# Encoder trunk on one core: the rotary angle arithmetic moves from the vector engine to Pool

## The chip, the cores and the metric

The kernel runs on one core of one Trainium2 chip. The metric is device time in microseconds of one execution. The engines are named as in the profile: PE (TensorE, matrix products), DVE (VectorE), ACT (ScalarE), POOL (GpSimd) and SP (SyncE, which issues most transfers). Each engine works through a queue of its own, in order; engines wait for each other through semaphores.

## The reference

Two layers; x is 512 tokens by 1024. Each layer mixes tokens (latent attention with rotary positions beside a gated convolution), attends to a memory of 256 rows, and ends in a gated feed-forward part. The change concerns the angles of the rotary positions:

```python
def rope_cos_sin(positions, dim):
    inv_freq = ROPE_BASE ** (-jnp.arange(0, dim, 2, dtype=jnp.float32) / dim)
    ang = positions.astype(jnp.float32)[..., None] * inv_freq
    return jnp.cos(ang), jnp.sin(ang)

def hybrid_mixer(x, cos, sin, ...):
    proj = x @ w_in + b_in
    c_q, c_kv, k_r, u = ...
    y_att = mla_group(c_q, c_kv, k_r, cos, sin, ...)
    y_conv = conformer_conv_group(u, ...)
    return jnp.concatenate([y_att, y_conv], axis=-1) @ w_o
```

Positions go up to 4606, so an angle has to be brought into one turn with more than float32's bits before a sine is taken. There are 16 angles for each of 512 positions, and the tables are used by both layers.

## The kernel before, in words

**Products.** Every float32 operand is split into a high and a low part (`whi`, `wlo`; `xTh`, `xTl`), and each product is three matmuls (`mm3`, L250 to L252). Weights arrive in a raw buffer (three of them), ACT casts the high part (L225, L304) and DVE (L226) or POOL (L312) subtracts it to get the low part. The raw buffer is free for the next fetch once the low part is made.

**Start of the program.** x comes in four tiles of 128 tokens. `transpose_x` (L412 to L422) turns a tile on PE, ACT makes `xTh` and DVE `xTl`. The gated unit's input projection is cut into eight blocks of 128 features. `blocks[0].first`, `blocks[1].first` and `blocks[2].first` compute blocks 0 to 2 for the first two token tiles (24 products of 128x256 each) as soon as these are there, while tiles 2 and 3 are still being turned; the second half of each block follows in the mixer. DVE splits the weights of blocks 0 to 2, POOL those of blocks 3 to 7 and of the latents (`wc`).

**Rotary tables.** `rope_tables` (L337 to L394) stands behind this. It casts the positions (`posi`, fetched by POOL's queue), multiplies them with 16 frequencies, splits the angle, multiplies it by 1/(2 pi) in parts of 12 bits and takes off whole turns by casting to integer and back (`whole`, L360 to L363). `tot` is then the angle in turns between -0.5 and 0.5. Seven more operations fold it for the sine and the cosine, and ACT takes `Sin` of both. All of it works on tiles `ropew` of 128x64 on DVE, each step on the result of the one before. POOL only fills in the frequencies.

**The mixer and its order.** The steps of layer 0's mixer are generators: each yields its engine, an estimated cost and the buffers and events that it needs. `Weave` is a list scheduler that emits them in the order in which it estimates that they could start. `issue_order` ties the instructions traced inside it to trace order on each engine; between the start and the mixer, which are two such sections, the tile framework may still interleave. Among the mixer's steps are the rest of the eight blocks (`gates`), the gate (ACT `th`, L650, then DVE `ch`, L652), the convolution with 31 taps on DVE (L616; one of four groups on ACT and POOL, L605 and L607), the transposes of the memory rows `mem` (L537), fetched by SP between the weights, and the latents (`latent`), which first use the tables (L711).

**Constants of a layer.** `mixer` begins with the fetches of `vec` and `cbias` on POOL's queue and with `hvec`, half of some of `vec` (L579 to L586).

Of the kernel before, what the change touches and what calls it, by code (L numbers as in the profile page):

```python
# [8 lines left out]
F32 = mybir.dt.float32  # L9
# [8 lines left out]
P = 128  # L18
# [25 lines left out]
SCRATCH = 9  # L44
POOL_TILES = (1,)
# [6 lines left out]
# ROPE_BASE ** (-arange(0, 32, 2) / 32) in float32  # L52
# [6 lines left out]
# 1 / (2 pi) in parts of 12 bits  # L59
TURN_BITS = 0x28BE60DB9391054A7F09  # floor(2**80 / (2 pi)), leading digits in hex  # L60
# [8 lines left out]
class Weave:  # L69
    """Emits the steps of several generators in the order in which a list scheduler would start them.  # L70

    A generator yields what its next step needs and emits that step when it is resumed. Steps of one generator
    follow each other; `get` and `put` count buffers, `wait` and `fire` order steps of different generators.
    """
# [82 lines left out]
@contextmanager  # L157
def issue_order(tc, engines):
    """Instructions traced inside are issued in trace order on each of the engines."""
    nc = tc.nc  # L160
    traced = nc.cur_bb.bb.instructions
    last = traced[-1]
    yield
    start = next(k for k in reversed(range(len(traced))) if traced[k] is last) + 1
    prev = {}
    for i in traced[start:]:
        if i.engine in engines:
            if i.engine in prev:
                tc.add_manual_dep(i, prev[i.engine].name,
                                  mybir.DependencyInfo(mybir.DependencyClass.NoSync, mybir.DependencyReason.DATA),  # L170
                                  reason="issue order")
            prev[i.engine] = i
# [3 lines left out]
def encoder(ctx: ExitStack, tc: tile.TileContext, x_in, mem_in, pos_in, wu, wc, wuq, wukv, wo,  # L176
# [45 lines left out]
    def split(src, hi, lo, scale=None):  # L222
        """hi + lo == src (times scale), hi and lo of 12 significant bits each."""
        if scale is None:
            nc.scalar.copy(hi, src)  # L225
            nc.vector.tensor_tensor(lo, src, hi.bitcast(F32), op=ALU.subtract)  # L226
        else:
            nc.scalar.activation(hi, src, AF.Copy if isinstance(scale, float) else AF.Identity, scale=scale)
            nc.vector.scalar_tensor_tensor(out=lo, in0=src, scalar=scale, in1=hi.bitcast(F32),
                                           op0=ALU.mult, op1=ALU.subtract)  # L230
# [17 lines left out]
    def mm3(o, l, r, first, last):  # L248
        """o += l^T r for split operands; lo * lo is below float32's last bit."""
        nc.tensor.matmul(o, l[0], r[0], start=first, stop=False)  # L250
        nc.tensor.matmul(o, l[0], r[1], start=False, stop=False)  # L251
        nc.tensor.matmul(o, l[1], r[0], start=False, stop=last)  # L252
# [7 lines left out]
    def blk(i, n=P):  # L260
        return slice(i * n, (i + 1) * n)
# [20 lines left out]
    class Unit:  # L282
        """A piece of weights on its way: fetched, then split, lo on DVE or on Pool."""
# [50 lines left out]
    cosT = const.tile([P, NT, 16], F32, name="cosT")  # L334
    sinT = const.tile([P, NT, 16], F32, name="sinT")

    def rope_tables():  # L337
        posi = const.tile([P, NT], I32, name="posi")
        nc.gpsimd.dma_start(out=posi, in_=pos_in)
        posf = const.tile([P, NT], F32, name="posf")  # L340
        nc.vector.tensor_copy(posf, posi)
        work = bigt([P, 16, 64], F32, name="ropew")
        used = iter(range(16))

        def t64():
            return work[:, next(used), :]

        ang, freq = t64(), t64()
        for i in range(16):
            nc.gpsimd.memset(freq[:, i:i + 1], INV_FREQ[i])  # L350
        for t in range(NT):
            nc.vector.tensor_scalar(ang[:, blk(t, 16)], freq[:, 0:16], posf[:, t:t + 1], None, op0=ALU.mult)
        ah = small.tile([P, 64], F32R, name="ah", bufs=1)
        nc.vector.tensor_copy(ah, ang)
        al = t64()
        nc.vector.tensor_tensor(al, ang, ah.bitcast(F32), op=ALU.subtract)
        ahf = ah.bitcast(F32)
        n, m, pr = t64().bitcast(I32), t64(), t64()

        def whole(dst, src):  # L360
            nc.vector.tensor_copy(n, src)
            nc.vector.tensor_copy(m, n)
            nc.vector.tensor_tensor(dst, src, m, op=ALU.subtract)  # L363

        tiny = t64()
        nc.vector.tensor_scalar(tiny, ahf, TURN_PARTS[5], None, op0=ALU.mult)
        for src, i in ((al, 4), (ahf, 4), (al, 3), (al, 2), (ahf, 3)):
            nc.vector.scalar_tensor_tensor(out=tiny, in0=src, scalar=TURN_PARTS[i], in1=tiny,
                                           op0=ALU.mult, op1=ALU.add)
        tot = t64()  # L370
        for first, (src, i) in enumerate(((ahf, 0), (al, 0), (ahf, 1), (al, 1), (ahf, 2))):
            nc.vector.tensor_scalar(pr, src, TURN_PARTS[i], None, op0=ALU.mult)
            if first == 0:
                whole(tot, pr)
            else:
                whole(pr, pr)
                nc.vector.tensor_tensor(tot, tot, pr, op=ALU.add)
                whole(tot, tot)
        nc.vector.tensor_tensor(tot, tot, tiny, op=ALU.add)
        hop = t64()  # L380
        nc.vector.tensor_scalar(hop, tot, 0.5, None, op0=ALU.is_gt)
        nc.vector.tensor_tensor(tot, tot, hop, op=ALU.subtract)
        nc.vector.tensor_scalar(hop, tot, -0.5, None, op0=ALU.is_lt)
        nc.vector.tensor_tensor(tot, tot, hop, op=ALU.add)
        a1, a2 = t64(), t64()
        nc.vector.tensor_scalar(a1, tot, -1.0, 0.5, op0=ALU.mult, op1=ALU.add)
        nc.vector.tensor_tensor(a1, a1, tot, op=ALU.min)
        nc.vector.tensor_scalar(a2, tot, -1.0, -0.5, op0=ALU.mult, op1=ALU.add)
        nc.vector.tensor_tensor(a1, a1, a2, op=ALU.max)
        nc.scalar.activation(sinT.rearrange("p t f -> p (t f)"), a1, AF.Sin, scale=TWO_PI)  # L390
        nc.vector.tensor_scalar(a2, tot, -1.0, None, op0=ALU.mult)
        nc.vector.tensor_tensor(a2, a2, tot, op=ALU.min)
        nc.vector.tensor_scalar(a2, a2, 0.25, None, op0=ALU.add)
        nc.scalar.activation(cosT.rearrange("p t f -> p (t f)"), a2, AF.Sin, scale=TWO_PI)  # L394

# [47 lines left out]
    class Norm:  # L443
        """x <- LayerNorm(ALPHA x + y) of one token tile, y arriving in two halves."""
# [22 lines left out]
    class Block:  # L467
        """128 output features of x W, feature-major over all the tokens."""
# [28 lines left out]
    def tail(x, gb, half0, mm, blocks, keep=None):  # L497
        """Token tiles leave one by one: product, norm, transposes; the next blocks start on the first tiles."""
# [23 lines left out]
    mkv = [dram.tile([XH, P, 1024], F32, name=f"mkv{l}") for l in range(DEPTH)]  # L522

    def memory_kv(l, wk, wv, begin, stored):
        """Steps; wk and wv are weight units."""
# [51 lines left out]
    def mixer(l, xT, blocks, x_src):  # L577
        v = vecp.tile([P, 148], F32, name="vec")
        nc.gpsimd.dma_start(out=v, in_=vec[l])  # L579
        hv = vecp.tile([P, 136], F32, name="hvec")  # L580
# [4 lines left out]
        cbias = scr(name="cbias")  # L585
        nc.gpsimd.dma_start(out=cbias, in_=row[l, 6:7, 0:CIN].partition_broadcast(P))  # L586

        # depthwise causal convolution, summed in a PSUM bank
# [32 lines left out]
        # gated linear unit, twice its value  # L621
# [25 lines left out]
        def gated_steps(m):  # L647
# [12 lines left out]
                   q=2, gate=2)  # L660

        # latents, token-major
# [15 lines left out]
        def latent(t):  # L678
# [28 lines left out]
            yield pool(1.5, fire=roped[t])  # L707
# [35 lines left out]
        # keys of two heads, feature-major: own 64 rows, then rotary and mask rows  # L743
# [22 lines left out]
        # queries of two heads, token-major for the rotation, then feature-major  # L766
# [37 lines left out]
        # values, token-major  # L804
# [10 lines left out]
        # attention: one item is a query tile of one head, or of both while they share a bank  # L815
# [76 lines left out]
        # channel norm and swish of the convolution, a token tile at a time  # L892
# [225 lines left out]
    xs = dram.tile([SEQ, D], F32, name="xs")  # L1118
    blocks = mixer_blocks(0)
# [6 lines left out]
    with issue_order(tc, ORDERED):  # L1126
        for t in range(2):
            transpose_x(x[t], t, xT)
        blocks[0].first(xT)
        blocks[1].load()  # L1130
        transpose_x(x[2], 2, xT)
        blocks[1].first(xT)
        blocks[2].load()
        transpose_x(x[3], 3, xT)
        blocks[2].first(xT)
        rope_tables()
    for l in range(DEPTH):
        x, xT, blocks = mixer(l, xT, blocks, x_in if l == 0 else xs)
# [73 lines left out]
```

## Time and profile before

| what | value |
|---|---|
| runs | 1493.42, 1491.61 and 1491.92 us, median 1491.92 |
| profiled execution, from first to last instruction | 1492.6 us (this span is the time that the profile gives for it) |
| PE busy | 1452.6 us, 97% |
| DVE busy | 856.7 us, 57% |
| ACT busy | 597.8 us, 40% |
| POOL busy | 358.1 us, 24% |
| DVE in 25 to 50 us | 24.21 of 25 us |
| PE in 50 to 75 us | 16.15 of 25 us |

The shares are means over stages with different limits. Around the change, in the first 100 us, DVE is busy nearly all the time from 25 us on, and PE is not. A busy PE is not PE at its peak: matmuls overlap, so what counts is the distance from one start to the next.

### The profile page before, as it was taken

Reading aid. Unit: us, or ns where it says so; the run is one execution under the profiler, and the core shown is the slowest. Engines: PE = TensorE matmul, PEld = TensorE weight load, DVE = VectorE, ACT = ScalarE, POOL = GpSimd, SP = SyncE. Lnnn points to the kernel's source line nnn. Section 1 sums busy time; section 2 is a strip of 40 time slices with the busy share of each in tenths; the row PEclk is TensorE's granted clock in tenths of the full one; section 3 lists DMA queues with packets and bytes.
Section 4 is the critical chain, followed back from the end, with each engine's and each line's share of the span. In section 5 each row is a group of like instructions: output and inputs, shape, how many; then the busy total and the mean of one; then the engine's idle time right before and its main releaser. Section 6 shows DMA issues by size and latency. Waiting matters only on the chain.

```text
span 1492.6 us, 20901 instructions
## 1 busy us (share of the span) xinstructions
PE 1452.6 (97%) x8152; PEld 1255.0 (84%) x8152; DVE 856.7 (57%) x1313; ACT 597.8 (40%) x1152; POOL 358.1 (24%) x539
## 2 busy tenths in 40 slices
PE   8799999999999999999999999999999999999997
PEld 7699988988888888888888998888888888888886
DVE  6999677665733333442469886785665333336215
ACT  4577773453322222331146777624523222225210
POOL 2679771000200000000147877510010000000001
PEclk9899999999999999999999999999999999999999
DMA  5325344242233233333233444422414233333211
GB/s 179 127 82 169 103 128 155 85 156 70 99 113 96 91 104 99 99 99 99 85 114 123 128 121 129 162 71 99 156 43 150 92 98 99 99 99 98 92 51 57
DMA packets 46306, 161.18 MB, mean 108 GB/s; under 512 B 5312, under 2 KB 5344, under 8 KB 46208
## 3 DMA queue, kind: packets, MB, share of 16 engines
q1 hardware_dynamic: 43616, 150.75, 31.4%
q0 software_dynamic: 2592, 9.10, 1.9%
q8 instruction: 64, 1.05, 0.3%
q14 instruction: 34, 0.28, 0.1%
HBM read 147.25 MB, written 8.39 MB: 104 GB/s over the span
## 4 chain that ended last, share of the span: by engine, by line
PE 73%; DVE 11%; DMA 5%; ACT 5%; POOL 4%; issue 3%; SPq 0%; POOLq 0%; DVEq 0%; ACTq 0%
PE accb L251 18%; PE accb L250 18%; PE accb L252 18%; PE psb L250 5%; PE psb L251 5%; PE psb L252 5%; DMA raw<-in_xo 3%; DVE convb L616 2%; DVE wlo L226 2%; DVE p L846 1%; POOL wlo L312 1%; DMA raw<-in_xq 1%; ACT whi L225 1%; PE convb L250 1%; PE convb L251 1%
## 5 line engine op out<-in xcount | busy, mean ns | idle before, releaser
L226 DVE TENSOR_TENSOR wlo<-raw,whi 128x1024 fp32r<-128x1024 f32 (+1 forms) x175 | 210.8, 1207 | 351.2 <-ACT whi L225 350.1
L251 PE MATMUL accb<-xTl,whi 128*128 128x512 f32 (+1 forms) x1104 | 400.8, 364 | 1.8 <-DVE xTl L422 1.7
L250 PE MATMUL accb<-xTh,whi 128*128 128x512 f32 (+1 forms) x1104 | 400.1, 365 | 1.5 <-ACT whi L225 1.3
L252 PE MATMUL accb<-xTh,wlo 128*128 128x512 f32 (+1 forms) x1104 | 399.8, 363 | 0.3 <-DVE wlo L226 0.3
L225 ACT CAST whi<-raw 128x1024 fp32r<-128x1024 f32 (+1 forms) x175 | 182.1, 1042 | 540.6 <-PE accb L251 333.2
L251 PEld LDWEIGHTS accb<-xTl,whi 128*128 128x128 f32 x1104 | 209.5, 190 | 34.7 <-DVE xTl L422 3.4
L250 PEld LDWEIGHTS accb<-xTh,whi 128*128 128x128 f32 x1104 | 208.2, 190 | 35.8 <-ACT xTh L419 2.6
L252 PEld LDWEIGHTS accb<-xTh,wlo 128*128 128x128 f32 x1104 | 209.6, 190 | 32.6 <-DVE wlo L226 0.6
L436 POOL TENSOR_SCALAR ve<-mv 128x1 f32<-128x1 f32 x32 | 27.5, 861 | 749.4 <-DVE mv L457 740.3
L312 POOL TENSOR_TENSOR wlo<-raw,whi 128x1024 fp32r<-128x1024 f32 (+1 forms) x63 | 152.6, 2424 | 59.5 <-ACT whi L304 59.3
L616 DVE SCALAR_TENSOR_TENSOR convb<-ch,hvec,convb 128x511 f32<-128x511 f32 (+9 forms) x180 | 132.5, 736 | 5.2 <-ACT convb L613 1.7
L1088 DVE SCALAR_TENSOR_TENSOR hid<-scr,accb 128x512 f32<-128x512 f32 x44 | 30.3, 688 | 109.8 <-PE accb L252 109.6
L607 POOL TENSOR_TENSOR cs<-cs,scr 128x511 f32<-128x511 f32 (+29 forms) x60 | 71.1, 1184 | 36.3 <-ACT scr L605 34.9
L250 PE MATMUL accb<-whi,hs 128*128 128x512 f32 x176 | 68.6, 390 | 0.0
L304 ACT CAST whi<-raw 128x1024 fp32r<-128x1024 f32 (+1 forms) x63 | 66.7, 1060 | 4.5 <-PE accb L252 1.7
L252 PE MATMUL accb<-whi,hs 128*128 128x512 f32 x176 | 68.5, 389 | 0.0
L251 PE MATMUL accb<-wlo,hs 128*128 128x512 f32 x176 | 68.5, 389 | 0.0
L252 PE MATMUL psb<-whi,hs 128*128 128x512 f32 x132 | 51.4, 389 | 0.0
L250 PE MATMUL psb<-whi,hs 128*128 128x512 f32 x132 | 51.3, 389 | 0.0
L251 PE MATMUL psb<-wlo,hs 128*128 128x512 f32 x132 | 51.3, 389 | 0.0
L419 ACT CAST xTh<-psb 128x256 fp32r<-128x256 f32 x64 | 20.1, 383 | 66.4 <-PE psb L416 66.0
L605 ACT ACTIVATE scr<-ch,hvec 128x511 f32<-128x511 f32 (+29 forms) x60 | 42.9, 716 | 0.0
(291 smaller groups left out, 2979.2 us busy)
## 6 DMA issues: line engine op xcount, KB each, us to landing
raw<-in_fin SPq DMA_DIRECT2D x88, 512.0 KB, 3.5
raw<-in_fdn SPq DMA_DIRECT2D x44, 512.0 KB, 3.5
raw<-in_xk SPq DMA_DIRECT2D x16, 512.0 KB, 3.6
raw<-in_xv SPq DMA_DIRECT2D x16, 512.0 KB, 3.6
raw<-in_wo SPq DMA_DIRECT2D x16, 512.0 KB, 3.6
raw<-in_xq SPq DMA_DIRECT2D x16, 512.0 KB, 3.6
raw<-in_xo SPq DMA_DIRECT2D x16, 512.0 KB, 3.6
raw<-in_wu SPq DMA_DIRECT2D x13, 512.0 KB, 3.3
```

The lines of the kernel that those rows point to most:

```text
L225: nc.scalar.copy(hi, src)
L226: nc.vector.tensor_tensor(lo, src, hi.bitcast(F32), op=ALU.subtract)
L250: nc.tensor.matmul(o, l[0], r[0], start=first, stop=False)
L251: nc.tensor.matmul(o, l[0], r[1], start=False, stop=False)
L252: nc.tensor.matmul(o, l[1], r[0], start=False, stop=last)
L304: nc.scalar.copy(hi, raw)
L312: eng.tensor_tensor(lo, raw, hi.bitcast(F32), op=ALU.subtract)
L436: nc.gpsimd.tensor_scalar(v, src, eps, None, op0=ALU.add)
L605: nc.scalar.activation(part, src[:, :SEQ - d], AF.Identity, scale=tap(m, d))
L607: nc.gpsimd.tensor_tensor(o[:, d:], o[:, d:], part, op=ALU.add)
L616: nc.vector.scalar_tensor_tensor(out=o[:, d:], in0=src[:, :SEQ - d], scalar=tap(m, d), in1=o[:, d:], op0=ALU.mult, op1=ALU.add)
L1088: nc.vector.scalar_tensor_tensor(out=hid[j // 2][:, j % 2, :], in0=th, scalar=0.5, in1=ou, op0=ALU.mult, op1=ALU.mult)
```

## The change

The arithmetic from the positions to `tot` is put on POOL (`nc.gpsimd`) and traced ahead of the transposes; the five fused multiply-adds become ten instructions, since they are written as a product and a sum there. The seven folds stay on DVE and the two sines on ACT, but as steps `rope_steps` of the mixer's list scheduler, which is told that POOL is free and the angles are there 4.0 us after its start (`ROPE_LATE`). The latents' rotation waits for their event `tabled`. The fetch of the positions goes to the head of POOL's queue, and layer 0's `vec` and `cbias` are fetched before x is.

```diff
+    posi = const.tile([P, NT], I32, name="posi")
+    nc.gpsimd.dma_start(out=posi, in_=pos_in)
     ident = const.tile([P, P], F32, name="ident")
...
     def rope_tables():
-        posi = const.tile([P, NT], I32, name="posi")
-        nc.gpsimd.dma_start(out=posi, in_=pos_in)
         posf = const.tile([P, NT], F32, name="posf")
-        nc.vector.tensor_copy(posf, posi)
+        nc.gpsimd.tensor_copy(posf, posi)
...
-            nc.vector.tensor_scalar(ang[:, blk(t, 16)], freq[:, 0:16], posf[:, t:t + 1], None, op0=ALU.mult)
+            nc.gpsimd.tensor_scalar(ang[:, blk(t, 16)], freq[:, 0:16], posf[:, t:t + 1], None, op0=ALU.mult)
...
         def whole(dst, src):
-            nc.vector.tensor_copy(n, src)
-            nc.vector.tensor_copy(m, n)
-            nc.vector.tensor_tensor(dst, src, m, op=ALU.subtract)
+            nc.gpsimd.tensor_copy(n, src)
+            nc.gpsimd.tensor_copy(m, n)
+            nc.gpsimd.tensor_tensor(dst, src, m, op=ALU.subtract)
...
         for src, i in ((al, 4), (ahf, 4), (al, 3), (al, 2), (ahf, 3)):
-            nc.vector.scalar_tensor_tensor(out=tiny, in0=src, scalar=TURN_PARTS[i], in1=tiny,
-                                           op0=ALU.mult, op1=ALU.add)
+            nc.gpsimd.tensor_scalar(pr, src, TURN_PARTS[i], None, op0=ALU.mult)
+            nc.gpsimd.tensor_tensor(tiny, tiny, pr, op=ALU.add)
...
+        def fold_sin():
+            nc.vector.tensor_scalar(a1, tot, -1.0, 0.5, op0=ALU.mult, op1=ALU.add)
+            nc.vector.tensor_tensor(a1, a1, tot, op=ALU.min)
+            nc.vector.tensor_scalar(a2, tot, -1.0, -0.5, op0=ALU.mult, op1=ALU.add)
+            nc.vector.tensor_tensor(a1, a1, a2, op=ALU.max)
+            nc.vector.tensor_scalar(a2, tot, -1.0, None, op0=ALU.mult)
+            nc.vector.tensor_tensor(a2, a2, tot, op=ALU.min)
+            nc.vector.tensor_scalar(a2, a2, 0.25, None, op0=ALU.add)
+
+        def sines():
+            nc.scalar.activation(sinT.rearrange("p t f -> p (t f)"), a1, AF.Sin, scale=TWO_PI)
+            nc.scalar.activation(cosT.rearrange("p t f -> p (t f)"), a2, AF.Sin, scale=TWO_PI)
+
+        rope_rest.extend((fold_sin, sines))
...
+        def rope_steps(turned):
+            yield dve(64, 7, 150, wait=(turned,), lag=0.1)
+            fold, sines = rope_rest
+            rope_rest.clear()
+            fold()
+            yield act(64, 2, 1500, fire=tabled)
+            sines()
...
+        if rope_rest:
+            turned = Event()
+            turned.time = wv.clock["POOL"] = ROPE_LATE
+            wv.add(0, rope_steps(turned))
+        else:
+            tabled.time = 0.0
...
-            yield pool(1.5, fire=roped[t])
+            yield pool(1.5, wait=(tabled,), fire=roped[t])
...
+    constants = mixer_constants(0)
     blocks = mixer_blocks(0)
...
     with issue_order(tc, ORDERED):
+        rope_tables()
         for t in range(2):
             transpose_x(x[t], t, xT)
...
         blocks[2].first(xT)
-        rope_tables()
```

Three places show where the instructions now stand. On DVE, at the start of the program, before (L422 makes `xTl`, L226 `wlo` of blocks 0 to 2 in two pieces each, L341 is the first instruction of the tables):

```order
L422 TENSOR_TENSOR xTl<-convb,xTh 128x2x128 x2
L226 TENSOR_TENSOR wlo<-raw,whi 128x512 x4
L422 TENSOR_TENSOR xTl<-psb,xTh 128x2x128 x4
L226 TENSOR_TENSOR wlo<-raw,whi 128x512 x2
L422 TENSOR_TENSOR xTl<-psb,xTh 128x2x128 x2
```

and in the changed kernel (L432 and L227 are these two lines there, L392 to L398 the seven folds):

```order
L432 TENSOR_TENSOR xTl<-convb,xTh 128x2x128 x2
L227 TENSOR_TENSOR wlo<-raw,whi 128x512 x4
L392 TENSOR_SCALAR ropew<-ropew 128x64
L393 TENSOR_TENSOR ropew<-ropew 128x64
L394 TENSOR_SCALAR ropew<-ropew 128x64
L395 TENSOR_TENSOR ropew<-ropew 128x64
L396 TENSOR_SCALAR ropew<-ropew 128x64
L397 TENSOR_TENSOR ropew<-ropew 128x64
L398 TENSOR_SCALAR ropew<-ropew 128x64
L432 TENSOR_TENSOR xTl<-psb,xTh 128x2x128 x4
L227 TENSOR_TENSOR wlo<-raw,whi 128x512 x2
```

The folds stand between the weights of block 1 and token tile 2; in the kernel before, all of the tables came behind tile 3.

On POOL, before, behind the constants (L312 is the split of block 3's weights and the next):

```order
L586 DMA cbias<-in_row 128x544
L581 TENSOR_SCALAR hvec<-vec 128x136
L350 MEMSET ropew 128x1 x16
L312 TENSOR_TENSOR wlo<-raw,whi 128x1024 x4
```

and in the changed kernel, with the pattern of the tables' steps cut short (L388 is the last of them, L313 the split):

```order
L591 DMA cbias<-in_row 128x544
L345 CAST posf<-posi 128x4
L354 MEMSET ropew 128x1 x16
L356 TENSOR_SCALAR ropew<-ropew,posf 128x16 x4
L358 CAST ah<-ropew 128x64
...
L597 TENSOR_SCALAR hvec<-vec 128x136
...
L387 TENSOR_SCALAR ropew<-ropew 128x64
L388 TENSOR_TENSOR ropew<-ropew 128x64
L313 TENSOR_TENSOR wlo<-raw,whi 128x1024 x4
```

Twelve of the 59 steps stand ahead of `hvec` and 47 behind it; the first weight split comes after all of them.

On SP, the fetches around `mem`, as a difference:

```order
-L266 DMA raw<-in_wc 128x1088 x3
-L532 DMA mem<-in_mem 128x1024
-L266 DMA raw<-in_wc 128x1088
+L267 DMA raw<-in_wc 128x1088 x2
+L542 DMA mem<-in_mem 128x1024
+L267 DMA raw<-in_wc 128x1088 x2
```

The first fetch of `mem` stands behind two fetches of `wc` and no longer behind three. In layer 1 the order of PE, DVE, ACT and SP is that of before.

## Rows read from the trace of the kernel before

**Rows 1.** Page, part 1: busy us, share of the span, instructions.

```profile
PE 1452.6 (97%) x8152; PEld 1255.0 (84%) x8152; DVE 856.7 (57%) x1313; ACT 597.8 (40%) x1152; POOL 358.1 (24%) x539
```

**Rows 2.** Stretches of 10 us: length, busy us of each engine, clock, DMA.

```profile
50.00:60.00 10.00, 1.15 (x6) 1.12 (x6) 9.75 (x13) 8.65 (x13) 8.42 (x6) 0.72 0.41 146
60.00:70.00 10.00, 10.00 (x40) 8.13 (x40) 9.16 (x13) 5.48 (x9) 9.50 (x6) 0.77 0.52 176
```

**Rows 3.** Timeline of PE: start us, us, line, tiles [idle before it].

```profile
19.20 0.36 PE L250 MATMUL accb<-xTh,whi 128*128 128x256 f32 x1
...
19.41 0.28 PE L251 MATMUL accb<-xTl,whi 128*128 128x256 f32 x1
...
19.52 0.28 PE L252 MATMUL accb<-xTh,wlo 128*128 128x256 f32 x1
...
58.88 1.12 PE L537 MATMUL psb<-ident,mem 128*128 128x128 f32 x4 [8.85 <-DMA mem<-in_mem]
```

**Rows 4.** Chain of waits, 0 to 150 us: start us, us on the chain, what.

```profile
11.54 0.21 PE accb L251
...
21.33 0.66 DVE ropew L352 x4
...
50.58 0.94 ACT whi L304
51.59 2.35 POOL wlo L312
...
54.34 4.49 DMA mem<-in_mem
...
60.85 0.43 PE accb L252
...
66.16 0.23 PE accb L250
```

**Rows 5.** Timeline of DVE, 15 to 30 us.

```profile
15.98 1.42 DVE L422 TENSOR_TENSOR xTl<-psb,xTh 128x256 fp32r<-128x256 f32 x4 [1.59 <-ACT xTh L419]
17.32 1.28 DVE L226 TENSOR_TENSOR wlo<-raw,whi 128x512 fp32r<-128x512 f32 x2
...
24.24 0.20 DVE L362 CAST ropew<-ropew 128x64 f32<-128x64 int32 x1
24.47 0.22 DVE L363 TENSOR_TENSOR ropew<-ropew 128x64 f32<-128x64 f32 x1
...
26.99 2.41 DVE L362 CAST ropew<-ropew 128x64 f32<-128x64 int32 x1
```

**Rows 6.** Timeline of POOL, the start and around 89 us.

```profile
9.83 0.59 POOL L581 TENSOR_SCALAR hvec<-vec 128x136 f32<-128x136 f32 x1 [5.45 <-DMA vec<-in_vec]
10.37 0.53 POOL L350 MEMSET ropew<- 128x1 f32 x16
26.95 2.40 POOL L312 TENSOR_TENSOR wlo<-raw,whi 128x1024 fp32r<-128x1024 f32 x1 [16.05 <-ACT whi L304]
...
89.42 0.26 POOL L711 TENSOR_TENSOR ra<-ctok,cosT 128x32 f32<-128x32 f32 x1
89.63 0.27 POOL L712 TENSOR_TENSOR rb<-ctok,sinT 128x32 f32<-128x32 f32 x1
89.97 0.23 POOL L714 TENSOR_TENSOR kx<-ra,rb 128x16 f32<-128x16 f32 x1
```

**Rows 7.** DMA issues, 0 to 70 us: count, KB, median us to landing.

```profile
posi<-in_pos POOLq DMA_DIRECT2D x1, 2.0 KB, 5.7
```

**Rows 8.** Groups of POOL by shape, whole span: count, busy us, mean ns, idle before.

```profile
L312 POOL TENSOR_TENSOR wlo<-raw,whi 128x1024 fp32r<-128x1024 f32 x55 | 131.9, 2400 | 58.6 <-ACT whi L304 58.4
...
L781 POOL COPY qs<-maskp 128x64 f32<-128x64 f32 x32 | 8.0, 256 | 0.7 <-DVE yc L243 0.6
...
L714 POOL TENSOR_TENSOR kx<-ra,rb 128x16 f32<-128x16 f32 x16 | 3.6, 223 | 0.6
...
L438 POOL TENSOR_SCALAR ve<-ss 128x2 f32<-128x2 f32 x8 | 1.5, 192 | 6.3 <-ACT scr L701 6.0
```

More of the change, by code (lines that the diff above doesn't have):

```diff
@@ L44 @@
 SCRATCH = 9
+ROPE_LATE = 4.0
 POOL_TILES = (1,)
@@ L335, in encoder @@
     sinT = const.tile([P, NT, 16], F32, name="sinT")
+    rope_rest = []
     def rope_tables():
-        posi = const.tile([P, NT], I32, name="posi")
-        nc.gpsimd.dma_start(out=posi, in_=pos_in)
         posf = const.tile([P, NT], F32, name="posf")
-        nc.vector.tensor_copy(posf, posi)
+        nc.gpsimd.tensor_copy(posf, posi)
         work = bigt([P, 16, 64], F32, name="ropew")
@@ L351, in rope_tables @@
         for t in range(NT):
-            nc.vector.tensor_scalar(ang[:, blk(t, 16)], freq[:, 0:16], posf[:, t:t + 1], None, op0=ALU.mult)
+            nc.gpsimd.tensor_scalar(ang[:, blk(t, 16)], freq[:, 0:16], posf[:, t:t + 1], None, op0=ALU.mult)
         ah = small.tile([P, 64], F32R, name="ah", bufs=1)
-        nc.vector.tensor_copy(ah, ang)
+        nc.gpsimd.tensor_copy(ah, ang)
         al = t64()
-        nc.vector.tensor_tensor(al, ang, ah.bitcast(F32), op=ALU.subtract)
+        nc.gpsimd.tensor_tensor(al, ang, ah.bitcast(F32), op=ALU.subtract)
         ahf = ah.bitcast(F32)
@@ L360, in whole @@
         def whole(dst, src):
-            nc.vector.tensor_copy(n, src)
-            nc.vector.tensor_copy(m, n)
-            nc.vector.tensor_tensor(dst, src, m, op=ALU.subtract)
+            nc.gpsimd.tensor_copy(n, src)
+            nc.gpsimd.tensor_copy(m, n)
+            nc.gpsimd.tensor_tensor(dst, src, m, op=ALU.subtract)
         tiny = t64()
-        nc.vector.tensor_scalar(tiny, ahf, TURN_PARTS[5], None, op0=ALU.mult)
+        nc.gpsimd.tensor_scalar(tiny, ahf, TURN_PARTS[5], None, op0=ALU.mult)
         for src, i in ((al, 4), (ahf, 4), (al, 3), (al, 2), (ahf, 3)):
-            nc.vector.scalar_tensor_tensor(out=tiny, in0=src, scalar=TURN_PARTS[i], in1=tiny,
-                                           op0=ALU.mult, op1=ALU.add)
+            nc.gpsimd.tensor_scalar(pr, src, TURN_PARTS[i], None, op0=ALU.mult)
+            nc.gpsimd.tensor_tensor(tiny, tiny, pr, op=ALU.add)
         tot = t64()
         for first, (src, i) in enumerate(((ahf, 0), (al, 0), (ahf, 1), (al, 1), (ahf, 2))):
-            nc.vector.tensor_scalar(pr, src, TURN_PARTS[i], None, op0=ALU.mult)
+            nc.gpsimd.tensor_scalar(pr, src, TURN_PARTS[i], None, op0=ALU.mult)
             if first == 0:
@@ L376, in rope_tables @@
                 whole(pr, pr)
-                nc.vector.tensor_tensor(tot, tot, pr, op=ALU.add)
+                nc.gpsimd.tensor_tensor(tot, tot, pr, op=ALU.add)
                 whole(tot, tot)
-        nc.vector.tensor_tensor(tot, tot, tiny, op=ALU.add)
+        nc.gpsimd.tensor_tensor(tot, tot, tiny, op=ALU.add)
         hop = t64()
[L381 to L384, printed above, removed]
+        nc.gpsimd.tensor_scalar(hop, tot, 0.5, None, op0=ALU.is_gt)
+        nc.gpsimd.tensor_tensor(tot, tot, hop, op=ALU.subtract)
+        nc.gpsimd.tensor_scalar(hop, tot, -0.5, None, op0=ALU.is_lt)
+        nc.gpsimd.tensor_tensor(tot, tot, hop, op=ALU.add)
         a1, a2 = t64(), t64()
[L386 to L394, printed above, removed]
+        def fold_sin():
[10 more added lines that the diff above has]
+        rope_rest.extend((fold_sin, sines))
     def load_x(src, tiles=range(NT), pieces=1):
@@ L575, in mixer_blocks, with mixer_constants, mixer @@
         return [Block(wu[l, (m % 2) * 4 + m // 2], m >= 3) for m in range(8)]
-    def mixer(l, xT, blocks, x_src):
+    def mixer_constants(l):
         v = vecp.tile([P, 148], F32, name="vec")
         nc.gpsimd.dma_start(out=v, in_=vec[l])
+        cbias = scr(name="cbias")
+        nc.gpsimd.dma_start(out=cbias, in_=row[l, 6:7, 0:CIN].partition_broadcast(P))
+        return v, cbias
+    def mixer(l, xT, blocks, x_src, constants):
+        v, cbias = constants
         hv = vecp.tile([P, 136], F32, name="hvec")
@@ L583, in mixer @@
         b_g2, cg2, cb2, taps = hv[:, 0:4], hv[:, 4:8], hv[:, 8:12], hv[:, 12:136]
-        cbias = scr(name="cbias")
-        nc.gpsimd.dma_start(out=cbias, in_=row[l, 6:7, 0:CIN].partition_broadcast(P))
         ch = [bigt([P, 2, SEQ], F32, name="ch") for _ in range(2)]
@@ L619, in convolution @@
             nc.scalar.copy(summed[m], o)
+        tabled = Event()
+        def rope_steps(turned):
[5 more added lines that the diff above has]
+            sines()
         def block_steps(b, unit):
@@ L1135, in encoder @@
         blocks[2].first(xT)
-        rope_tables()
     for l in range(DEPTH):
-        x, xT, blocks = mixer(l, xT, blocks, x_in if l == 0 else xs)
+        if l:
+            constants = mixer_constants(l)
+        x, xT, blocks = mixer(l, xT, blocks, x_in if l == 0 else xs, constants)
         xT, blocks = cross(l, x, xT, blocks)
```

## The prediction

> **What bounds the kernel now.** I read the page first: TensorE (PE) is busy 1452.6 of 1492.6 us [rows 1], so what can be won or lost lies in the 40 us in which it is not, and in stretches at a lower clock. Then the busy time by stretches of 10 us: one hole stands out, 50 to 60 us, in which PE is busy 1.15 us [rows 2]. The granted clock is 0.72 there and 0.77 in the next 10 us, against 1.00 elsewhere: PE rested, and part of what follows runs at 1.2 GHz instead of 2.4. PE's timeline names the wait: at 58.88 the transposes of the memory rows had waited 8.85 us for a transfer [rows 3].
>
> Then the chain of waits, followed back from that transfer [rows 4]: the fetch of `mem` (4.49 us) starts when a raw buffer comes free, by POOL's fifth split (`wlo`, 51.59), which needed ACT's cast (50.58), which stood in ACT's queue behind convolution and sine steps that waited for DVE, and DVE worked through the rotary angles (`ropew`) from 21.33. Some of these took ten times their usual length: the CAST at 26.99 ran 2.41 us, the one at 24.24 0.20 [rows 5], while POOL's split ran from 26.95 for 2.40 [rows 6]. So the angles on DVE are on the path that sets the hole. The change takes them away from there; the question is what it puts in their place.
>
> The loss to be beaten is 8.85 us idle plus the slow clock behind it: 12 matmuls at 0.43 us each instead of 0.23 [rows 4], 2.4 us, and 4 transposes, some 0.5 us. Together 11.75 us.
>
> **The change part by part.**
>
> *POOL's chain.* 59 small instructions now run on POOL, each on the result of the one before, beside 16 fills that POOL had already. In the middle, behind 12 of them, stands `hvec`, which waits for `vec`: in the trace POOL got to it at 9.83 and finished 0.59 later [rows 6], so 10.4. The 12 before it are hidden by that wait if the positions land soon: worked out with the prices below they and the fills (0.53, [rows 6]) take 4.6 us. The position fetch took 5.7 us from its issue [rows 7]; it now issues some 1.5 us earlier, at about 0.7, at the head of POOL's queue. If it keeps its 5.7 us, the 12 end at 11.0 and `hvec` at 11.6. I take 10.4 and keep 11.6 as the other end.
>
> After `hvec` come 47: 19 with two inputs, 10 with a scalar, 18 casts, all 128x64. No row has a two-input operation of this size. Between 128x16 (223 ns) and 128x1024 (2400 ns) [rows 8] the slope is 2.16 ns per element: 223 + 48 x 2.16 = 327 ns. A dependent instruction starts 0.07 us after its predecessor's end (89.63 + 0.27 to 89.97, [rows 6]). So 0.40 us each, 7.6 us for 19. For the other 28 the near end is POOL's COPY of exactly this size, 256 ns; the far end comes from the scalar operations, 192 ns at 128x2 [rows 8] and 594 ns at 128x136 [rows 6], 3.0 ns per element: 378 ns. I take the middle, 317 ns, since no row says to which of the two an immediate scalar and a cast to integer belong; with the 0.07 that is 0.39 each, 10.9 us (9.1 to 12.5). The chain ends at 10.4 + 7.6 + 10.9 = **28.9 us** (27.1 to 30.5; 31.7 with the late positions).
>
> *DVE's queue.* The seven folds that read the chain's result do not stand at the end of this stage. They stand directly behind the splits of blocks 0 and 1, ahead of the splits of token tile 2, of block 2's weights and of tile 3 (the first of the places shown with the change). DVE works in its queue's order. Where DVE went on to tile 2 at 15.98 and to block 2's `wlo` at 17.32 [rows 5], it now waits for POOL until 28.9. Then seven folds at 0.23 from start to start [rows 5] = 1.6; four `xTl`, 1.42; half of block 2's `wlo`, 0.64; with 0.15 to the next engine, 3.8 us. Block 2's first product can start at **32.7 us**. Before, it started at 19.20 [rows 3]. PE has nothing else: block 1's first product and the transposes of tile 3 are done by then, and all that follows in its queue is behind block 2. That is 13.5 us of idle PE, where before there was none.
>
> *The clock behind it.* After the idle stretch at 50 us the products were slow at 60.85 and at full pace only at 66.16 [rows 4]; the products at the kernel's start also ran slow (0.21 per 128x256 product at 11.54 [rows 4] against 0.11 to 0.12 at 19.41 [rows 3]). The 24 products of block 2 then cost 24 x 0.09 = 2.2 us extra. Loss in the new place: 15.7 us.
>
> *The old hole.* Counted from PE's restart, ACT's and POOL's work is driven by the block products (24 of 128x256 at 0.12, of 128x512 at 0.23, the first 24 at 0.21). Block 0 is done at +8.0; with one ACT step, the cast and POOL's 2.40 the split of block 3 is done at +12.5 (PE needs it at +13.7), block 4's at +18.0 (+19.2) although the sines with their table loads now stand ahead of it, block 5's at +20.4 (+24.6), block 6's at +25.4 (+30). SP's queue has the fetch of `mem` now behind two `wc` fetches and not three, so behind block 6's split and no longer behind block 7's: issued at about +26, landed at +30.7 by the 4.49 us of the row. PE wants it behind 84 products of 128x512, at +32.7, which is 65 us. So the hole at 50 us closes, and its 11.75 us are gained, with 2 us to spare.
>
> *The rest.* DVE is relieved of 54 instructions and of the long stops beside POOL's splits; its convolution starts later, behind block 1's gate, but has no angles between its taps, so that it is about as far on when PE comes to `mem`. The list scheduler gives the rest of layer 0's mixer another order, which no row prices: PE is the engine that is busy there, so I put it at 0 and keep 2 us each way. POOL's constants and the fetches of `vec` and `cbias` move by about one DMA issue; `hvec`, their first user, is in the sum, and what PE waits for at the start is the fetch of `x`: 0. From the end of layer 0's mixer on, every engine's order is the same: 0.
>
> **The sum**: 15.7 - 11.75 = **+4.0 us** on the profiled span of 1492.6 us, in short: the end of POOL's chain minus 24.9. The median of the runs is 0.7 us below that span; 1491.9 + 4.0 = 1495.9, say 1496. A measurement of this kernel tells about 0.2%, 3 us, from no change.
>
> **The Trainium skill against the rows.** The CAST of 2.41 us [rows 5] shows that POOL's and DVE's operations can exclude each other. The Trainium skill's page "SBUF — State Buffer" (section "Who interferes with whom") says that a DVE instruction with two SBUF inputs and a GpSimd instruction that reads SBUF block each other for a whole instruction, whichever began first. The time by such a lock, from rows: four DVE `wlo` pieces of blocks 0 and 1 (0.64 each, as in [rows 5]) stand ahead of the folds, beside POOL's chain; if POOL stands still for each, the chain ends 2.6 us later. By that rule the sum is +6.6; without it, +4.0.
>
> **The rivals.**
> 1. *POOL goes at its independent pace: faster.* Two operations that don't read each other start 0.21 us apart though each lasts 0.26 (89.42, 89.63, [rows 6]). If the chain went so, 47 x 0.21 = 9.9, it ended at 20.3: -4.6 us, 1487.3. It decides at 21.9 (0.245 per instruction): below that, the kernel is faster by over 0.2%, since the hole of 8.85 us closes and the new one is smaller. Against it: every step reads the one before, and such pairs show the 0.07 us on top of the whole duration.
> 2. *Half-way: no change.* POOL keeps its durations but the 0.07 between dependent steps disappears (47 x 0.07 = 3.3): chain to between 23.8 and 26, -1 to +1 us, about 1492. For it: the 0.21 us of rival 1. Against it: the 0.07 is in the row of the dependent pair.
> 3. *The lock on the splits*, as above: +6.6, 1498.5; with the upper prices, +8.2. For it: the 2.41 us. Against it: most of the chain runs while DVE only waits.
> 4. *A new wait at the latent products.* PE's new order takes 18 of them, which need the third `wc`, before block 7; POOL's split of it comes some 1.6 us late by the same count: +5.6, 1497.5. For it: POOL's splits of 2.40 us follow each other closely. Against it: the same count leaves 1 to 4 us of room at the blocks before.
>
> **How the numbers follow.** The forecast's case (chain to 27 to 32 us, rival 4 included) has 0.50; its own range is +2 to +7, 1494 to 1499; of it I count 0.12 below the 3 us of the measurement. Rival 1 has 0.20, rival 2 0.23, rival 3 0.07. Slower: 0.38 + 0.07 = 0.45; same: 0.12 + 0.23 = 0.35; faster: 0.20. The range runs from 1488, inside rival 1, to 1501, which takes in rival 3 with the upper prices and a little of the rest: it leaves out some 0.13 below and 0.05 above.
>
> **What would show it.** Right: DVE's first fold (L392) waits some 14 us for POOL's last angle (L388, ending near 29); PE is idle from 19 to about 33 before block 2's first products, with a clock near 0.5 after it; no wait for `mem` near 65; layer 1 as before. Wrong: folds that start before 22 us (rival 1), POOL's 128x64 operations well under 0.25 us, DVE's `wlo` pieces stretched to a microsecond (rival 3), or PE still waiting for `mem`, in which case the old hole was not closed and the time would be near 1507.

## The result, and the profile after

The changed kernel takes 1507.59 us (median of 4 runs, 1504.38 to 1508.04), the kernel before 1491.99. The ratio is 1.0095 (1.0081 to 1.0109), which is 14.2 us slower (12.1 to 16.3); the two medians lie 15.6 us apart. The direction was forecast, the size was not: the forecast was +4 us, with a range up to 1501. The profiled execution has a span of 1506.1 us.

Differences below are ratios times 1492 us, the median of before; each ratio compares runs on one chip, the kernel before among them, and stands with its 95% interval.

The page, part 1, of the changed kernel (it answers to [rows 1]):

```profile
PE 1454.8 (97%) x8152; PEld 1257.1 (83%) x8152; DVE 844.0 (56%) x1259; ACT 596.3 (40%) x1152; POOL 379.1 (25%) x598
```

PE's busy time grew by 2.2 us; the other 11.3 of the 13.5 us by which the span grew are time in which PE rests. POOL's timeline (start us, us; compare [rows 6, 8]):

```profile
10.51 0.88 POOL L597 TENSOR_SCALAR hvec<-vec 128x136 f32<-128x136 f32 x1
...
15.17 0.24 POOL L366 CAST ropew<-ropew 128x64 f32<-128x64 int32 x1
15.49 0.32 POOL L367 TENSOR_TENSOR ropew<-ropew 128x64 f32<-128x64 f32 x1
15.90 0.37 POOL L376 TENSOR_SCALAR ropew<-ropew 128x64 f32<-128x64 f32 x1
...
29.02 0.32 POOL L388 TENSOR_TENSOR ropew<-ropew 128x64 f32<-128x64 f32 x1
```

The chain ends at 29.3. DVE's timeline at the same place (it answers to [rows 5]):

```profile
12.70 1.47 DVE L227 TENSOR_TENSOR wlo<-raw,whi 128x512 fp32r<-128x512 f32 x2 [1.72 <-ACT whi L226]
29.37 0.20 DVE L392 TENSOR_SCALAR ropew<-ropew 128x64 f32<-128x64 f32 x1 [15.20 <-POOL ropew L388]
...
30.82 1.41 DVE L432 TENSOR_TENSOR xTl<-psb,xTh 128x256 fp32r<-128x256 f32 x4
32.15 1.28 DVE L227 TENSOR_TENSOR wlo<-raw,whi 128x512 fp32r<-128x512 f32 x2
```

DVE stands for 15.2 us in front of the first fold, with tile 2 and block 2's weights behind it. PE's timeline shows what that does, and that the memory rows no longer make it wait (they answer to [rows 3]):

```profile
32.88 0.58 PE L253 MATMUL accb<-xTh,wlo 128*128 128x256 f32 x1 [13.11 <-DVE wlo L227]
...
65.60 0.60 PE L547 MATMUL psb<-ident,mem 128*128 128x128 f32 x4
```

The stretches of 10 us (as in [rows 2]) show the hole at its new place and the clock in and behind it, 0.72 and 0.59, a good part of the time at the lower level:

```profile
20.00:30.00 10.00, 0.00 (x0) 0.00 (x0) 0.56 (x4) 0.34 (x2) 7.49 (x26) 0.72 0.00 0
30.00:40.00 10.00, 7.12 (x40) 7.12 (x41) 4.66 (x14) 0.00 (x0) 0.00 (x0) 0.59 0.16 54
```

Up to here the forecast holds within half a microsecond: chain to 29.3 (forecast 28.9), restart of PE at 32.9 (32.7), `mem` wanted at 65.6 (65) and there. So the other 10 us lie behind 65 us. The busy time from 60 to 290 us (length, then PE, PEld, DVE, ACT, POOL), in the changed kernel and in the kernel before:

```profile
60.00:290.00 230.00, 216.93 (x1575) 197.47 (x1574) 188.47 (x310) 142.25 (x338) 149.74 (x221) 0.99 0.38 124
```

```profile
60.00:290.00 230.00, 225.09 (x1654) 205.99 (x1654) 181.85 (x312) 143.72 (x342) 139.91 (x217) 0.99 0.39 122
```

PE rests 13.1 us in this stretch where it rested 4.9; up to 60 us it rests 3.0 us longer than before, and behind 290 us as long as before. PE's waits from 62 to 300 us (line, releaser, total us, times, longest) show many small ones:

```profile
PE accb L251 <- DVE qTl L246: 3.5, 2, 2.5
PE accb L252 <- DVE pl L244: 2.4, 1, 2.4
PE psb L251 <- DVE mTl L244: 1.9, 1, 1.9
PE accb L253 <- POOL wlo L313: 1.3, 1, 1.3
PE accb L829 <- POOL qs L826: 1.3, 2, 0.7
PE psb L880 <- DVE p L875: 1.1, 3, 0.7
```

The same view of the kernel before:

```profile
PE psb L851 <- DVE p L846: 2.4, 5, 0.9
PE accb L251 <- DVE pl L243: 0.9, 3, 0.4
PE psb L537 <- DVE mTl L243: 0.4, 1, 0.4
```

### The profile page after: what moved, and what is told of

Read it like the earlier page. It is cut to its first block, busy times and chain, and to the rows that moved or that the text cites. A ratio compares the mean times of both kernels' runs of the same rounds, so it can differ in the third digit from the quotient of the medians.

```text
span 1506.1 us, 20908 instructions
## 1 busy us (share of the span) xinstructions
PE 1454.8 (97%) x8152; PEld 1257.1 (83%) x8152; DVE 844.0 (56%) x1259; ACT 596.3 (40%) x1152; POOL 379.1 (25%) x598
## 4 chain that ended last, share of the span: by engine, by line
PE 79%; DVE 7%; DMA 4%; ACT 4%; POOL 3%; issue 2%; POOLq 0%; DVEq 0%; ACTq 0%
PE accb L252 19%; PE accb L251 19%; PE accb L253 19%; PE psb L251 5%; PE psb L252 5%; PE psb L253 5%; DMA raw<-in_xo 3%; DVE wlo L227 1%; DVE p L875 1%; PE psb L880 1%; ACT whi L226 1%; DMA raw<-in_xq 1%; PE convb L251 1%; PE convb L253 1%; PE convb L252 1%
## 5 line engine op out<-in xcount | busy, mean ns | idle before, releaser
L253 PE MATMUL accb<-xTh,wlo 128*128 128x512 f32 (+1 forms) x1104 | 400.5, 363 | 13.2 <-DVE wlo L227 13.1
L227 DVE TENSOR_TENSOR wlo<-raw,whi 128x1024 fp32r<-128x1024 f32 (+1 forms) x175 | 210.9, 1207 | 350.6 <-ACT whi L226 349.3
L226 ACT CAST whi<-raw 128x1024 fp32r<-128x1024 f32 (+1 forms) x175 | 181.7, 1040 | 542.1 <-PE accb L252 333.3
L253 PEld LDWEIGHTS accb<-xTh,wlo 128*128 128x128 f32 x1104 | 210.4, 191 | 45.7 <-DVE wlo L227 13.7
L313 POOL TENSOR_TENSOR wlo<-raw,whi 128x1024 fp32r<-128x1024 f32 (+1 forms) x63 | 152.3, 2419 | 61.9 <-ACT whi L305 61.8
L305 ACT CAST whi<-raw 128x1024 fp32r<-128x1024 f32 (+1 forms) x63 | 67.0, 1064 | 5.0 <-POOL cs L620 1.6
L875 DVE TENSOR_SCALAR p<-p,ri 128x128 f32<-128x128 f32 (+3 forms) x64 | 44.7, 718 | 2.1
```

Of the source, the lines that this page charges most:

```text
L305: nc.scalar.copy(hi, raw)
L313: eng.tensor_tensor(lo, raw, hi.bitcast(F32), op=ALU.subtract)
L875: nc.vector.tensor_scalar(p[:, blk(i, nk)], p[:, blk(i, nk)], ri[:, i:i + 1], None, op0=ALU.mult)
```

## The experiments

Two theories for the missing 10 us. Theory 1: the folds and sines, booked as steps, give the list scheduler another order of the whole mixer of layer 0, and that order is worse. Theory 2: the order is harmless; DVE and POOL come out of the hole too late and pass that on. The hole and the order can be changed apart, which makes a square of four kernels; the changed kernel is its fourth corner.

A step that is told to the list scheduler is booked: it takes estimated time on an engine, and steps behind it move. In these kernels the folds and sines are emitted inside other steps, so that the scheduler need not know of them (the comments say where the lines stand):

```diff
+            if m == 1 and late.get("fold"):      # at the end of gated_steps(1)
+                late.pop("fold")()
...
+                if d == 1 and late.get("sines"):  # in conv_pool, after the first tap on ACT
+                    late.pop("sines")()
```

**The hole kept, the old order.** The fold is emitted between block 1's and tile 2's splits, the list scheduler has no step for the tables:

```diff
         blocks[1].load()
+        late.pop("fold")()
         transpose_x(x[2], 2, xT)
...
-        if rope_rest:
+        if False:
```

> The angles stay on Pool and the folds stay on DVE ahead of token tile 2's splits (the hole at 19 to 33 us is kept), but the list scheduler knows nothing of the tables: the layer-0 mixer has the order of the kernel before on every engine, with the folds and sines hung into it. Theory 1 (the new list order of the mixer costs about 10 us, the hole as forecast +4): 1494 to 1498 us. Theory 2 (the order is harmless, DVE and Pool come out of the hole too late and pass that on): 1505 to 1509 us as in the changed kernel.

Measured: 1495.33 us, 1.0019 (1.0009 to 1.0028), +2.8 us. That is theory 1. Its PE has begun 256 matmuls by 65 us, the changed kernel's 258, so the two part behind that point; its matmuls stand in the order of before, all 8152 of them.

**No hole, the new order.** The bookings stay, the fold is emitted behind the second gate:

```diff
             yield dve(64, 7, 150, wait=(turned,), lag=0.1)
-            fold, sines = rope_rest
             rope_rest.clear()
-            fold()
             yield act(64, 2, 1500, fire=tabled)
-            sines()
```

> The mixer keeps the new list order, but the folds and sines are issued in the mixer behind the second gate, so DVE goes on to tile 2 without waiting for Pool. Theory 1: the hole at 19 to 33 us goes, the order's 10 us stay: 1490 to 1495 us. Theory 2: nearly all of the loss goes: 1480 to 1487 us.

Measured: 1495.43 us, 1.0019 (1.0003 to 1.0035), +2.8 us; 0.4 us above the range of theory 1 and far from theory 2. The matmuls stand in the changed kernel's order.

**Neither.** Both edits, the fold behind the second gate and no booking:

> Neither: angles on Pool, folds behind the second gate, the mixer's order of before. Both theories: about 1482 us (1479 to 1487): no hole at 19 us, the wait for the memory rows at 50 us closes (its 11.7 us), less some 2 us in which block 3's split waits for Pool's chain to end at 29. Theory 1 puts it about 10 us below the kernel with the new order, theory 2 within 3 us of it.

Measured: **1482.72 us, 0.9934 (0.9919 to 0.9949), 9.8 us faster than before.** This is the version to keep. PE's timeline in it, block 3's wait for POOL's chain and what is left of the wait for `mem`:

```profile
32.90 0.50 PE L253 MATMUL accb<-xTh,wlo 128*128 128x512 f32 x1 [1.60 <-POOL wlo L313]
...
52.24 0.66 PE L548 MATMUL psb<-ident,mem 128*128 128x128 f32 x4 [0.45 <-DMA mem<-in_mem]
```

The square, in us against the kernel before:

| | old order | new order | the order costs |
|---|---|---|---|
| no hole | -9.8 | +2.8 | 12.6 |
| hole | +2.8 | +14.2 | 11.4 |
| the hole costs | 12.6 | 11.4 | |

The intervals of two ratios make some 3 us either way for each of these differences. Within that the two costs add up, so neither needs the other. Taking the angles off DVE gains 9.8 us, the hole costs 11 to 13, and the order costs 11 to 13. What the hole costs is net: PE's waits for POOL's splits are 1.9 us in the kernel with neither and 0.3 in the one with the hole and the old order.

The busy time from 60 to 290 us shows the order's part as rest of PE. Old order, without the hole:

```profile
60.00:290.00 230.00, 224.53 (x1669) 206.09 (x1668) 180.22 (x313) 144.55 (x347) 132.67 (x213) 1.00 0.39 123
```

New order, without the hole:

```profile
60.00:290.00 230.00, 216.80 (x1595) 198.66 (x1594) 181.11 (x303) 138.62 (x336) 137.09 (x215) 0.98 0.37 117
```

PE rests 5.5 us in the one and 13.2 in the other, 7.7 us more; in the kernel with hole and old order it rests 4.6, against the changed kernel's 13.1. The two executions profiled here lie 16.1 us apart (1480.7 and 1496.8), since that of the new order took 3 us more than its median. Over the whole span PE rests 8.6 us longer in it, and the same 8152 matmuls keep PE busy 7.5 us longer (1456.3 and 1448.8), at a mean granted clock of 0.992 and not 0.999. The ten runs of the new order go the same way: 1488.17 us at a clock of 0.997, 1499.94 at 0.992. So the order costs rest, and on top of it time at the lower clock, which differs from run to run; no run shows the clock's part by itself.

**Another value for the number given to the scheduler.**

```diff
-ROPE_LATE = 4.0
+ROPE_LATE = 8.0
```

> The changed kernel with ROPE_LATE 8.0 in place of 4.0: the folds then stand behind tile 3's splits and the first gate, and the list scheduler gives a third order. Theory 1: anywhere from 1481 to 1496 us, by its order, and a difference of over 4 us from the other kernel without the hole and with a new order would itself show that the list order is worth several us. Theory 2: 1480 to 1487 us.

Measured: 1490.16 us, 0.9985 (0.9975 to 0.9994), -2.2 us. One number moves the folds behind tile 3's splits, gives a third order, and takes 16.4 us off the changed kernel. That is in the range of theory 1 and above that of theory 2; against the version with the old order it still loses 7.6 us.

**Does the order lose by scalings that meet POOL's splits?** In the kernel without the hole and with the new order, one of PE's two longest waits behind 17 us is 2.47 us for DVE at 129.66 (the other, 2.46 us, is for POOL's split at 33.39). DVE's timeline ahead of it:

```profile
121.96 2.80 DVE L877 TENSOR_SCALAR p<-p,ri 128x256 f32<-128x256 f32 x2
...
126.49 2.15 DVE L877 TENSOR_SCALAR p<-p,ri 128x384 f32<-128x384 f32 x1
128.56 0.73 DVE L632 SCALAR_TENSOR_TENSOR convb<-ch,hvec,convb 128x499 f32<-128x499 f32 x1
129.20 0.41 DVE L246 SCALAR_TENSOR_TENSOR qTl<-accb,qTh 128x256 fp32r<-128x256 f32 x1
```

and POOL's:

```profile
121.94 2.41 POOL L313 TENSOR_TENSOR wlo<-raw,whi 128x1024 fp32r<-128x1024 f32 x1
...
126.06 2.36 POOL L313 TENSOR_TENSOR wlo<-raw,whi 128x1024 fp32r<-128x1024 f32 x1 [0.22 <-ACT whi L305]
```

A scaling of 128x384 takes 2.15 us when it begins beside a split, and ends 0.2 us after the split. The Trainium skill's page "SBUF — State Buffer" (section "Who interferes with whom") counts `tensor_scalar` among the operations of DVE that can take the ports it shares with GpSimd, and says that the later one waits for the whole instruction; these rows agree. The good order has such meetings too: of a mixer's 32 scalings the longest took 1.90 us there and 2.60 here. Whether such meetings are the order's cost was tried by putting the scaling on ACT, in both orders:

```diff
-                nc.vector.tensor_scalar(p[:, blk(i, nk)], p[:, blk(i, nk)], ri[:, i:i + 1], None, op0=ALU.mult)
+                nc.scalar.activation(p[:, blk(i, nk)], p[:, blk(i, nk)], AF.Identity, scale=ri[:, i:i + 1])
```

> As the kernel without the hole and with the new order, but the scaling of the attention weights (L877) runs on ACT in the same place of the order, so that no DVE scaling can stand still behind a Pool split. If the new order is slow because these scalings meet Pool's splits (2.15 and 2.80 us instead of 0.42 to 0.69 in front of PE's wait of 2.47 us at 129.7), the distance to its twin with the old order shrinks from 12.7 to under 6 us. If the order is slow in itself, the distance stays above 9 us.

> The twin with the old order and the scaling on ACT. Expected within 3 us of the kernel without the hole and with the old order (1482.7), since DVE is relieved of 32 scalings and ACT has room.

Measured: 1496.88 us, 1.0030 (1.0017 to 1.0044), with the new order; 1488.55 us, 0.9979 (0.9968 to 0.9991), with the old. The distance is 7.6 us, between the two expectations, and the twin with the old order lost 6.7 us, which was not expected. The scalings' stalls beside POOL's splits are part of the order's cost at most; the new order is the slower one without them too.

**Which booking spoils the order, or does any other order lose?** ACT's booking alone:

```diff
-            yield dve(64, 7, 150, wait=(turned,), lag=0.1)
-            fold, sines = rope_rest
+            yield act(64, 2, 1500, wait=(turned,), fire=tabled)
             rope_rest.clear()
-            fold()
-            yield act(64, 2, 1500, fire=tabled)
-            sines()
```

> No hole; in the list scheduler only ACT's booking of the sines (3.1 us) is kept, DVE's booking is left out; this gives a fourth order. Booking theory (a booking of 3 us on ACT at the mixer's start is what spoils the order): 1492 to 1497 us. Chance theory (any other order lands anywhere): between 1482 and 1497.

Measured: 1492.74 us, 1.0010 (1.0000 to 1.0019), which both theories allow. The same with both bookings, 12 us later (`ROPE_LATE = 16.0`):

> No hole; both bookings kept, but ROPE_LATE 16.0, so that the list scheduler books the folds and sines 12 us later, after the first gates. A fifth order. Booking theory: nearer to the old order, 1482 to 1488 us, since the first gates and casts are no longer pushed. Chance theory: anywhere between 1482 and 1497.

Measured: 1502.03 us, 1.0075 (1.0050 to 1.0101): the slowest order of all, 14 us above the booking theory's range and 5 above that of chance, which was too narrow. The run does not leave the start alone, as was expected of it: ACT's second cast for POOL's splits (L305) starts at 31.94, behind the next block's activation, and not at 28.64, ahead of it, as in the old order. So the last two runs book nothing for the tables and only nudge a number of the scheduler in layer 0. `HOP` is its estimate, in us, for the way of a result from one engine to the next:

```diff
+        if l == 0:
+            wv.HOP = 0.17
```

> No hole, no booking of folds or sines; only the list scheduler's estimate of a hop between engines is 0.17 us and not 0.15 in layer 0, which gives yet another order of the mixer. If a booking for the tables is what spoils the order: within 4 us of the kernel without the hole and with the old order (1479 to 1487). If the old order is simply a good one among many and any nudge loses it: 1488 to 1500 us.

Measured: 1495.21 us, 1.0026 (1.0015 to 1.0036). `SLACK` says how much later than the earliest a step may start and still count as equal. With `wv.SLACK = 0.1`:

> The same with another nudge: steps within 0.10 us of the earliest, and not 0.05, count as equal in layer 0. Booking theory: 1479 to 1487 us. Any-nudge theory: 1488 to 1500 us.

Measured: 1492.76 us, 1.0007 (0.9997 to 1.0017). Both runs lie in the range for any nudge (1488 to 1500) and outside that for a booking (1479 to 1487): the booking theory falls.

All of these are without the hole, with the angles on POOL; the kernels differ in the mixer's order and, with it, in where the folds and sines fall:

| what the scheduler is told | order | against before, us | interval |
|---|---|---|---|
| nothing (old order) | 1 | -9.8 | -12.1 to -7.6 |
| tables at 8.0 | 2 | -2.2 | -3.7 to -0.9 |
| SLACK 0.10 for 0.05 | 3 | +1.0 | -0.4 to +2.5 |
| ACT's sines at 4.0 | 4 | +1.5 | 0.0 to +2.8 |
| tables at 4.0 | 5 | +2.8 | +0.4 to +5.2 |
| HOP 0.17 for 0.15 | 6 | +3.9 | +2.2 to +5.4 |
| tables at 16.0 | 7 | +11.2 | +7.5 to +15.1 |

The old order is the best of seven, by 7.6 us and more; orders 3 to 6 can hardly be told apart. A nudge of 0.02 us in an estimate that has nothing to do with the tables loses 13.7 us. The bookings bought one more such order and nothing else. The order with the other SLACK parts from the old one only behind 98 us, so that the start of the mixer need not be touched for a loss. Which step of an order decides is open: PE's waits are spread over many places and differ from order to order, and no single one was found that carries the difference.

## Why the prediction was wrong, point by point

**What held.** *POOL's chain*: forecast to 28.9, measured to 29.3. Two-input operations took 0.32 us (327 ns forecast), those with a scalar 0.37, near the upper of the two bounds (378 ns), and casts 0.24, just under the lower (256 ns). That the end came out so close is in part luck: the 18 casts and 10 scalar operations took 10.3 us together and not 10.9, and `hvec` ended at 11.4 and not 10.4. The positions had landed early enough (POOL's first step starts at 5.19), but the twelve steps and the fills took 5.2 us and not 4.6, and `hvec` then ran 0.88 us and not 0.59. *DVE's queue*: a wait of 15.2 us, PE idle for 13.1 us (13.5 forecast), restart at 32.9 (32.7). *The clock behind it*: PE started the 24 products of block 2 0.21 us apart, up to 38.0, and the next ones 0.12 apart, as forecast; only the remark that the clock of the kernel before was 1.00 elsewhere goes too far, since it was 0.83 from 10 to 20 us. *The old hole*: closed; `mem` had landed when PE came to it at 65.6. The kernel with the hole and the old order, which is the kernel that this part of the sum describes, lies +2.8 us (+1.3 to +4.2) from before; the sum said +4.0. Among the signs of being wrong the prediction named a time near 1507 for a hole that does not close. The measured 1507.6 is that figure by chance: the hole did close.

**What failed** is the step called *the rest*: "The list scheduler gives the rest of layer 0's mixer another order, which no row prices: PE is the engine that is busy there, so I put it at 0 and keep 2 us each way." Measured, 11 to 13 us. That PE is busy there was true of the old order, in which it rests 4.9 us in 230; another order need not keep it so. In the changed kernel it rests 13.1. A new order is not one more term with a small error: here it was as large as the hole, and the error was to treat the absence of a row as a small number.

**The rivals.** Rivals 1 and 2 did not occur: dependent steps started 0.06 to 0.09 us after their predecessor's end. Rival 3, the lock on the splits, is small: the two pairs of `wlo` pieces took 1.41 and 1.47 us (1.33 and 1.37 before). Beside them POOL's `hvec` ran 0.88 us (0.59 before) and three steps of the chain 0.56, 0.69 and 0.51 instead of 0.32 and 0.37: a microsecond in all, not 2.6. The rule that the prediction cites from the Trainium skill's page "SBUF — State Buffer" (section "Who interferes with whom") agrees in direction; POOL did not stand still for whole pieces, and no run shows why. Rival 4 put a wait of 1.6 us at the latents' products; there is one of 1.9 us, but for DVE's `mTl`, not for POOL's split.

## What to carry to other kernels

Look where an engine's queue puts the readers of a moved result: seven operations of 0.2 us, hoisted ahead of splits that PE needs, cost 11 to 13 us here, and behind them the same move gained 10. When a list scheduler works from estimates, a step that is told to it can redraw the whole order; here each of six small changes to its numbers did, and the redraw was a term as large as the change. Hang new work into existing steps first, keep the order, and measure the two apart. If an order must change, try several, and judge the change against the best.

## What was not expected of the hardware

A DVE scaling of 128x384 lasted 2.15 us (0.43 is the median of the scalings of all widths in the good order) beside a POOL split of 2.36 us, and moving all 32 of a mixer's scalings to ACT, in both layers, made the good order 6.7 us slower, not faster. One took 0.60 us on ACT (median); why that costs so much, with ACT busy 40% of the span, is not shown. On POOL a cast of 128x64 to or from integers took 0.24 us, and a multiplication by a constant 0.37 us, longer than an addition of two tensors (0.32).
